# Loading K of the first octet as two half-row transfers instead of one

## The chip, the cores and the metric

The kernel runs on one core of one Trainium2 chip. A core has a matrix engine (TensorE, PE in the profile), two engines for elementwise work (VectorE, DVE; ScalarE, ACT), a general engine (GpSimd, POOL), a synchronisation engine (SyncE, SP) and 16 DMA engines that move data between HBM and the on-chip SBUF. SP and POOL issue transfers; the DMA engines carry them out. The metric is the device time of one execution in microseconds (us), as the median of several runs.

## What is computed

Q, K and V have the shape 8 x 12 x 512 x 64 in float32: 96 heads of 512 rows of 64 numbers. Each head is a linear attention with ReLU features:

```python
Q_feat = np.maximum(0, Q)
K_feat = np.maximum(0, K)
KV = np.einsum('bhkd,bhkv->bhdv', K_feat, V)
K_sum = np.sum(K_feat, axis=2)
numerator = np.einsum('bhqd,bhdv->bhqv', Q_feat, KV)
denominator = np.einsum('bhqd,bhd->bhq', Q_feat, K_sum)
return (numerator / (denominator[:, :, :, None] + 1e-10)).astype(np.float32)
```

Each of Q, K, V and the output is 12.58 MB, so 37.75 MB are read and 12.58 MB written.

## The kernel before

**Tiles.** The 96 heads are cut into 12 octets of 8 heads (`NO = 12`). One octet of one tensor is 1 MB in float32 and is laid on 128 partitions, each of which gets one contiguous run of 32 rows (`RQ = 32`) of 64 numbers, which is 8 KB; a partition so holds rows of one head only, and a head covers 16 partitions.

**Loads.** The K and V of the first octet are loaded by SP as float32, into the tiles `k_first` and `v_first` (lines 105 to 109). They live in two buffers of the output pool (tag `o_sb`, 7 buffers), which is still empty then. Everything else is loaded by POOL, which converts to bfloat16 on the way: first Q of octet 0 (`load_q(0)`, line 110), then for each octet K, V and Q in this order (lines 113 to 127). Octets 1 to 8 (`N8 = 9`) are loaded in whole octets of 8 KB rows; K and V of the last three in halves of 4 KB rows (lines 125 and 126). All of POOL's loads are written at the start of its program; at most about eight of them are under way at once, since each one waits for an older one to land before it is issued.

**Work per octet.** `prep8_k` (line 155) takes the ReLU of one half of K on DVE and multiplies it by a mask, into two masked copies `kf`. `prep8_v` (line 161) writes masked copies of V to `vo_all`, partly on DVE (line 167) and partly on ACT (line 165). `mm_kv8` (line 169) multiplies the two on PE and accumulates over the 32 rows in PSUM; `evac_kv8` (line 179) copies the result to `kvd` on ACT. `qt` transposes Q on PE (line 224) and takes its ReLU on ACT (line 232). `denom` (line 271) makes the reciprocal of the denominators, `out_t` (line 246) the numerators, `back` (line 289) transposes them back, and `norm` (line 296) scales them on DVE into an `o_sb` tile that SP stores.

**Order.** The schedule is written by hand (`tc.manual_schedule()`): each engine runs its instructions in the order in which the code emits them, and the framework adds only the waits. On DVE the start is: the constant parts of `vo_all` (`zero8`, lines 145 and 147), the masks made from the identity matrix (lines 332 to 337), zeroing `kvd` (line 150), `zero_masks` (lines 132 to 135), and then, for both halves i of the first octet (lines 341 to 344):

```python
for i in range(2):
    prep8_k(0, i)
    prep8_v(0, i, 0, nc.vector)
    prep8_v(0, i, 1, nc.scalar)
```

`prep8_k(0, 0)` reads rows 0 to 15 of `k_first` on every partition, `prep8_k(0, 1)` rows 16 to 31; between the two stands `prep8_v(0, 0, 0)`, which reads `v_first`.

**Stores.** `store` (line 304) holds each store back: SP first issues a tiny transfer (a "probe", line 307) that reads from the K tile of the octet five further on (`DELAY = 5`), so it can only go out when that tile has landed, and then the store itself (line 315). The last octet's output goes out in two halves (line 313). The probes begin with the landing of octet 5, and so for the first third of the time the DMA engines only load.

Of the kernel before, what the change touches and what calls it, by code (L numbers as in the profile page):

```python
# [10 lines left out]
def kernel(  # L11
# [7 lines left out]
    nc = tc.nc  # L19
    B, H, S, D = Q.shape  # L20
# [6 lines left out]
    R = S * 4 // P  # L27
# [30 lines left out]
    def view(X, f):  # L58
        return X.rearrange("b h s d -> (b h s d)").rearrange("(n p f) -> n p f", p=P, f=f)
# [45 lines left out]
    K8, V8 = view(K, RQ * D), view(V, RQ * D)  # L105
    k8 = outp.tile([P, RQ, D], fp32, name="k_first", tag="o_sb")
    v8 = outp.tile([P, RQ, D], fp32, name="v_first", tag="o_sb")
    nc.sync.dma_start(out=k8.rearrange("p r d -> p (r d)"), in_=K8[0])
    nc.sync.dma_start(out=v8.rearrange("p r d -> p (r d)"), in_=V8[0])
    load_q(0)  # L110
    make_identity(nc, ident)
# [331 lines left out]
```

## Time and profile before

| what | value |
|---|---|
| three runs, median (lowest to highest) | 127.08 us (126.86 to 127.38) |
| the profiled execution, its own time | 127.24 us |
| its span, first to last instruction | 125.5 us |
| mean granted TensorE clock | 0.94 |
| busy: PE, DVE, ACT, POOL | 85.0, 82.0, 83.6, 23.5 us |
| DMA time on POOL's queue, as a share of 16 engines' span | 72.1% |
| DMA time on SP's queue, same measure | 28.8% |
| HBM traffic | 37.75 MB read, 12.58 MB written |
| issue to landing, median: V of the first octet | 9.4 us |
| issue to landing, median: Q, and whole K octets on POOL | 20.3 and 21.3 us |

The profiled execution took 127.24 us, of which 125.5 us lie between its first and last instruction; the 1.74 us around it are launch and end. Times inside the profile are counted from the span's start. A "window" row of the trace gives, for one stretch of time, the busy time of each engine with the number of its instructions, the granted PE clock, the mean busy share of the 16 DMA engines (which overlaps of consecutive packets carry a little above 1), and the rate in GB/s. That rate counts the bytes written at the destination: a POOL load reads 2 bytes of float32 for each byte of bfloat16 that it writes, so 213 GB/s there are 426 GB/s read. A timeline row gives start, duration, engine, line, operation, tiles and shape, and in square brackets how long the engine sat idle before it and what ended that.

### The profile page before, as it was taken

How to read it: one execution, taken by the hardware profiler on the slowest of the kernel's cores; microseconds unless marked ns; L12 is line 12 of the kernel's file. 1: busy time of each engine (PE TensorE's matmuls, PEld its weight loads, DVE VectorE, ACT ScalarE, POOL GpSimd, SP SyncE). 2: the span in 40 equal slices, each digit the busy share in tenths (PEclk: the TensorE clock that was granted, in tenths of full speed). 3: DMA queues.
4: the chain of work that ended last, by engine and by line, in shares of the span. 5: the costliest groups of instructions: out<-in, count | busy, mean ns of one | idle time of the engine just before them, and what ended most of it. 6: DMA issues, size and time to landing. Idle time of an engine off the chain costs nothing.

```text
span 125.5 us, 3277 instructions
## 1 busy us (share of the span) xinstructions
PE 85.0 (68%) x1363; PEld 76.0 (61%) x1363; DVE 82.0 (65%) x187; ACT 83.6 (67%) x146; POOL 23.5 (19%) x46
## 2 busy tenths in 40 slices
PE   0005829987879878798784995694497499597800
PEld 0005828966759667696672893593494498496700
DVE  2826519399594995949769337957909806988630
ACT  0006998899797997989967846966659446646300
POOL 6901131112311131011121111133111000000000
PEclk9999995999999999999999589999999959999975
DMA  3999999999999999999999999999999999999991
GB/s 99 376 319 218 214 217 217 208 214 215 212 216 212 214 217 235 316 222 253 323 230 239 320 242 227 356 210 249 338 212 232 334 233 219 359 411 428 431 384 63
DMA packets 8047, 32.72 MB, mean 261 GB/s; under 512 B 992, under 2 KB 992, under 8 KB 6368
## 3 DMA queue, kind: packets, MB, share of 16 engines
q0 software_dynamic: 5760, 17.83, 72.1%
q1 hardware_dynamic: 2272, 14.69, 28.8%
q8 instruction: 10, 0.16, 0.5%
q14 instruction: 5, 0.04, 0.1%
HBM read 37.75 MB, written 12.58 MB: 401 GB/s over the span
## 4 chain that ended last, share of the span: by engine, by line
DVE 31%; PE 28%; DMA 27%; issue 4%; ACT 4%; DVEq 1%; SPq 0%; ACTq 0%
DMA v_oct<-in_V_dram 19%; DVE o_sb L298 15%; PE ps_kv L173 9%; PE ps_bk L292 8%; DMA v_first<-in_V_dram 7%; PE ps_kv L203 4%; PE ps_qt L224 3%; DVE kf L189 2%; DVE own L277 2%; DVE den L282 2%; DVE kf L158 2%; DVE rec L286 2%; ACT kvd L183 2%; DVE vo_all L191 2%; PE ps_ot L254 1%
## 5 line engine op out<-in xcount | busy, mean ns | idle before, releaser
L298 DVE TENSOR_TENSOR o_sb<-ps_bk,rec 128x1024 f32<-128x1024 f32 x24 | 28.3, 1219 | 17.1 <-PE ps_bk L292 17.1
L224 PE MATMUL ps_qt<-ident,q_sb 128*128 128x128 bf16 x192 | 15.6, 247 | 12.3 <-DMA q_sb<-in_Q_dram 12.3
L173 PE MATMUL ps_kv<-vo_all,kf 64*128 64x132 bf16 x288 | 20.2, 229 | 5.2 <-DVE vo_all L167 4.8
L256 ACT COPY ot_sb<-ps_ot 128x1024 f32<-128x1024 f32 x22 | 21.5, 1015 | 3.3 <-PE ps_ot L254 3.0
L292 PE MATMUL ps_bk<-ident,ot_sb 128*128 128x128 f32 x192 | 23.4, 275 | 0.0
L173 PEld LDWEIGHTS <-kf 64*128 64x128 bf16 x576 | 18.7, 100 | 6.7 <-DVE vo_all L167 5.8
L232 ACT ACTIVATE qt<-ps_qt 128x1024 bf16<-128x1024 bf16 x23 | 22.4, 1031 | 0.5 <-PE ps_qt L224 0.4
L224 PEld LDWEIGHTS <-q_sb 128*128 128x128 bf16 x192 | 14.2, 113 | 12.9 <-DMA q_sb<-in_Q_dram 12.5
L292 PEld LDWEIGHTS ps_bk<-ident,ot_sb 128*128 128x128 f32 x192 | 20.9, 141 | 0.9
L173 PE MATMUL ps_den<-vo_all,kf 64*128 64x132 bf16 x288 | 20.2, 229 | 0.0
L158 DVE TENSOR_SCALAR kf<-k_oct,mask8k 128x1024 bf16<-128x1024 bf16 x32 | 13.4, 459 | 5.8 <-DMA k_oct<-in_K_dram 5.8
L254 PE MATMUL ps_ot<-qt,kvd 128*128 128x256 bf16 x88 | 13.6, 284 | 4.1 <-DVE o_sb L298 3.9
L183 ACT CAST kvd<-ps_kv 64x130 bf16<-64x130 f32 x36 | 9.5, 265 | 6.8 <-PE ps_den L173 6.1
L274 PEld LDWEIGHTS <-qt 128*128 128x128 bf16 x192 | 6.8, 97 | 9.2 <-issue 7.9
L254 PEld LDWEIGHTS <-kvd 128*128 128x128 bf16 x88 | 8.2, 101 | 6.8 <-issue 5.8
L274 PE MATMUL ps_den<-kvd,qt 128*128 128x16 bf16 x192 | 7.3, 179 | 7.2 <-ACT kvd L183 6.5
L213 ACT CAST kvd<-ps_kv 64x260 bf16<-64x260 f32 (+1 forms) x14 | 4.6, 328 | 9.0 <-PE ps_kv L203 8.4
L102 POOL DMA_DIRECT2D q_sb<-in_Q_dram x12 | 7.0, 584 | 18.5 <-DMA k_oct<-in_K_dram 12.6
L165 ACT ACTIVATE vo_all<-v_oct,mask 128x1024 bf16<-128x1024 bf16 x8 | 9.2, 1154 | 1.8 <-DMA v_oct<-in_V_dram 1.6
L203 PE MATMUL ps_kv<-vo_all,kf 128*128 128x132 bf16 x96 | 7.5, 237 | 4.1 <-DVE vo_all L198 3.6
L167 DVE TENSOR_SCALAR vo_all<-v_oct,mask 128x1024 bf16<-128x1024 bf16 x24 | 10.2, 481 | 0.0
L183 ACT CAST kvd<-ps_den 64x130 bf16<-64x130 f32 x36 | 9.5, 265 | 0.8
(40 smaller groups left out, 70.7 us busy)
## 6 DMA issues: line engine op xcount, KB each, us to landing
out_dram<-o_sb SPq DMA_DIRECT2D x11, 1024.0 KB, 9.0
q_sb<-in_Q_dram POOLq DMA_DIRECT2D x12, 512.0 KB, 20.3
k_oct<-in_K_dram POOLq DMA_DIRECT2D x8, 512.0 KB, 21.3
v_oct<-in_V_dram POOLq DMA_DIRECT2D x8, 512.0 KB, 20.3
k_oct<-in_K_dram POOLq DMA_DIRECT2D x6, 256.0 KB, 17.9
v_oct<-in_V_dram POOLq DMA_DIRECT2D x6, 256.0 KB, 16.9
k_first<-in_K_dram SPq DMA_DIRECT2D x1, 1024.0 KB
v_first<-in_V_dram SPq DMA_DIRECT2D x1, 1024.0 KB, 9.4
```

The lines of the kernel that those rows point to most:

```text
L158: nc.vector.tensor_scalar(kf[2 * o + i][:, :, s, :], kb[o][:, R * i:R * i + R], scalar1=0.0, scalar2=mask8k[:, s:s + 1], op0=Alu.max, op1= ...
L167: nc.vector.tensor_scalar(to, vb[o][:, rows], scalar1=mask[:, 0, t:t + 1], scalar2=None, op0=Alu.mult)
L173: nc.tensor.matmul(ps_row[i], kf[2 * o + r // R][ps, r % R, :, :].rearrange("p s d -> p (s d)"), vo8[o % 2][ps, r, :, 1:D4 - 1], start=(r ...
L183: nc.scalar.copy(kvd[o % NK][64 * c:64 * c + 64, 4 * i + s:4 * i + 4:2, c * D1:c * D1 + D1], ps_row[i][64 * s:64 * s + 64, :, c:c + D1])
L203: nc.tensor.matmul(ps_kv[:, g % 2, 0:2 * (D + 2)].rearrange("p (t d) -> p t d", t=2), kf[g][:, r, :, :].rearrange("p s d -> p (s d)"), vo[ ...
L224: nc.tensor.transpose(ps[:, u, :], q_sb[o][:, i * (U // 2) + u, :], ident)
L232: nc.scalar.activation(to, ps, Act.Relu)
L254: nc.tensor.matmul(ps[:, i], kvd[o % NK][:, h, 1:2 * D + 1], q[:, :, h, :], start=True, stop=True, skip_group_check=True)
L256: nc.scalar.copy(ot[o][:, :, 4 * j:4 * j + 4], ps.rearrange("p h u c -> p u h c"))
L274: nc.tensor.matmul(ps[:, u], qt_sb[o % NZ][:, u, :], kvd[o % NK][:, :, 0:2 * D1:2 * D1 - 1], start=True, stop=True, skip_group_check=True)
L292: nc.tensor.transpose(ps[:, 2 * v:2 * v + 2].rearrange("p c d -> p (c d)"), ot[o][:, 8 * j + v].rearrange("p h c -> p (h c)"), ident32)
L298: nc.vector.tensor_tensor(o_sb[:, rs], ps, rec[o][:, rs].unsqueeze(2).to_broadcast([P, 16, D]), op=Alu.mult)
```

## The change

K of the first octet is loaded by two transfers on SP. The first brings the first 4 KB of every partition's 8 KB (rows 0 to 15), the second the last 4 KB (rows 16 to 31). V follows as a third transfer on the same queue, in whole 8 KB rows as before. The tile, its place and all other instructions stay as they are.

```diff
-    nc.sync.dma_start(out=k8.rearrange("p r d -> p (r d)"), in_=K8[0])
+    for i in range(2):
+        rs = slice(R * D * i, R * D * i + R * D)
+        nc.sync.dma_start(out=k8.rearrange("p r d -> p (r d)")[:, rs], in_=K8[0][:, rs])
     nc.sync.dma_start(out=v8.rearrange("p r d -> p (r d)"), in_=V8[0])
     load_q(0)
```

`R * D` is 16 x 64 = 1024 numbers, or 4 KB.

## The prediction

> **What bounds the kernel now.** I read the 40 slices first. Each digit is the busy share of the 16 DMA engines in tenths; the numbers under it are GB/s at the destination.
>
> ```profile
> DMA  3999999999999999999999999999999999999991
> GB/s 99 376 319 218 214 217 217 208 214 215 212 216 212 214 217 235 316 222 253 323 230 239 320 242 227 356 210 249 338 212 232 334 233 219 359 411 428 431 384 63
> HBM read 37.75 MB, written 12.58 MB: 401 GB/s over the span
> ```
>
> The DMA engines are full from the second slice to the last but one, while no compute engine is busy for more than 68% of the span. The windows give the full rate (GB/s is the last column, DMA share the one before):
>
> ```profile
> 4.00:4.90 0.90, 0.00 (x0) 0.00 (x0) 0.83 (x4) 0.00 (x0) 0.90 (x3) 1.00 1.06 437
> 16.00:40.00 24.00, 18.96 (x347) 16.80 (x347) 16.50 (x35) 21.29 (x40) 5.37 (x10) 0.93 1.06 213
> 82.00:83.90 1.90, 1.90 (x46) 1.79 (x41) 0.97 (x3) 0.91 (x4) 0.74 (x1) 1.00 1.13 211
> 108.00:118.00 10.00, 8.66 (x119) 8.23 (x119) 8.10 (x18) 5.35 (x10) 0.00 (x0) 1.00 1.02 422
> 121.00:122.00 1.00, 0.00 (x0) 0.00 (x0) 0.00 (x0) 0.00 (x0) 0.00 (x0) 0.50 1.05 426
> ```
>
> Row 1 is SP's float32 load alone (437), row 2 POOL's loads of 8 KB rows (213 written, so 426 read), row 3 POOL's loads of 4 KB half rows (211, so 422 read), row 4 stores in 8 KB rows (422), row 5 the last store, in 4 KB rows (426). So all forms run at about 425 GB/s. The 37.75 + 12.58 = 50.33 MB need 118.1 us at 426 GB/s; the traffic lies between about 1.8 and 124.1 us, 122.3 us. The sum of DMA work is the bound, and its first and last 2 us are the only places where it is thin.
>
> The chain of waits says something else, and I don't follow it: it has "DMA v_oct" for 24.27 us from 59.51 on, and DVE and PE around it. Those 24 us are a queue of some eight transfers of about 2.5 us, so throughput again, and DVE's own rows show that compute caught up with the loads well before the end:
>
> ```profile
> 63.98 0.89 DVE L158 TENSOR_SCALAR kf<-k_oct,mask8k 128x1024 bf16<-128x1024 bf16 x2 [2.13 <-DMA k_oct<-in_K_dram]
> 73.86 0.88 DVE L158 TENSOR_SCALAR kf<-k_oct,mask8k 128x1024 bf16<-128x1024 bf16 x2 [3.67 <-DMA k_oct<-in_K_dram]
> 82.60 0.88 DVE L189 TENSOR_SCALAR kf<-k_oct,mask 128x1024 bf16<-128x1024 bf16 x2 [0.85 <-DMA k_oct<-in_K_dram]
> 83.81 0.49 DVE L191 TENSOR_SCALAR vo_all<-v_oct,mask 128x1024 bf16<-128x1024 bf16 x1 [0.33 <-DMA v_oct<-in_V_dram]
> ```
>
> DVE waits here for K of octets 7, 8 and 9 to land. A compute chain that starts up to 2.13 us later reaches 63.98 at the same time, and up to 2.13 + 3.67 = 5.80 us later it is level again at 73.86. The stores up to there hang on the probes, thus on landings, too.
>
> Now the start, where the change is:
>
> ```profile
> 0.74 0.39 SPq L108 DMA_DIRECT2D k_first<-in_K_dram  x1
> 1.19 0.42 SPq L109 DMA_DIRECT2D v_first<-in_V_dram  x1
> 1.24 0.66 POOL L102 DMA_DIRECT2D q_sb<-in_Q_dram  x1 [0.79 <-POOLq L427]
> 5.53 0.06 DVE L135 MEMSET mask<- 64x1 f32 x1
> 5.64 1.42 DVE L158 TENSOR_SCALAR kf<-k_first,mask8k 128x1024 bf16<-128x1024 f32 x2
> 10.60 0.75 DVE L167 TENSOR_SCALAR vo_all<-v_first,mask 128x1024 bf16<-128x1024 f32 x1 [3.54 <-DMA v_first<-in_V_dram]
> ```
>
> The first reader of K (L158 at 5.64) starts 0.05 us behind the last mask MEMSET (5.53 + 0.06 = 5.59) and shows no wait. By the trace's records of single DMA packets, which no view lists, K's packets run from 1.76 to 5.27 us, V's from 4.93 to 10.27, and Q's first one starts at 5.34. DVE then waits 3.54 us for V.
>
> **The change part by part.**
>
> *K's first half lands earlier: worth nothing.* Half of K would land near 4 us instead of 5.3. DVE has MEMSETs until 5.59, so at most 5.64 - 5.59 = 0.05 us could go, and then DVE would wait for V 0.05 us longer. The second half is first read by `prep8_k(0, 1)`, which stands behind the V work of 10.60 on DVE. Its new wait is met some 5 us earlier; behind it are queued the second V copy on DVE and, through `kf`, the second half of PE's products. I set it at 0, at most 0.05 us, covered by the 2.13 us at 63.98.
>
> *One more issue on SP.* It costs 0.39 us of SP's time, and V's issue moves from 1.19 to about 1.63. Nothing else stands on SP until the probe at 43.57, and POOL's queue is its own. V's issue would end near 2.05. K's first packets came 0.6 to 1.5 us behind the end of K's issue (1.13, to 1.76 and, on the last engine, 2.65), so V's would be ready between 2.7 and 3.6; K holds the engines until about 5. That is a cover of 1.4 us. The second K half is ready between 2.2 and 3.1; the first one holds the engines until about 3.7 (data flow from about 2.5, then 0.5 MB at 437 GB/s is 1.2 us). Cover: 0.6 us. So 0, with each us of a hole costing one us, since the DMA work is the bound.
>
> *128 rows become 256.* Each engine handles 16 pieces of 4 KB instead of 8 of 8 KB. The trace has no such load; the bounds come from its neighbours. Stores: 426 in 4 KB rows against 422, so nothing or a gain of 1%. POOL's loads: 211 against 213, so a loss of 1%. One MB at 426 GB/s is 2.46 us, so that is -0.02 to +0.02 us. By the packets' own records the loss is larger: 173 ns for a half row against 324 ns for a whole one is 22 ns for every extra piece, times 8 is 0.18 us; but these records overlap, and the window rate does not bear them out. Gains at the bottom end: a shorter first piece could bring the first data half a packet (309 ns / 2) earlier, -0.15. I take +0.03 (the loss of the nearest load, 0.02, and the 16 extra completion writes, one of 9 ns per engine); ends -0.15 and +0.18.
>
> *V beside Q.* From 5.34 on V and Q take turns, one packet each, so a K that ends 0.03 later puts V's end 0.03 to 0.06 later, and if V loses one turn on one engine, a Q packet of 0.32. DVE and PE then start up to 0.4 us later. That is under the 2.13 us of cover at 63.98: nothing. Without that cover it would be up to 0.4 us.
>
> A rule of the Trainium skill speaks against the change: "DMA: Bandwidth & Descriptors", section "Rules for kernel authors", advises at least 1 MiB in a DMA, and the section "Anatomy of one DMA" there gives a fixed cost of about 2.0 us for each. Were that paid in the queue, the sum would be about 2 us more. The trace speaks against paying it: V's first packets run at 4.93 us while K's last are still under way. "Perfetto Trace Analysis", section "DMA Optimizations", says for splitting that it may help if the DMA engines are generally idle; here they are not.
>
> *Sum.* +0.03 on the profiled execution's 127.24 gives 127.27. That execution lies 0.16 above the median of the three runs, 127.08; on the median I forecast 127.1.
>
> **The rivals.**
>
> *Slower: a hole in the DMA work at the start.* If the second half's pieces, or V's, come to the engines only when the transfer ahead is done, the engines stand idle between. Place: 3.7 us, and again at 5. Price: one us for each us, and the lag from issue to packets, 0.6 to 1.5 us, is the measure: 127.7 to 128.6. It decides when the lag of the second transfer exceeds its cover by over 0.6 us, that is beyond 1.2 us on all engines. For it: only four engines had packets at 1.76, the rest between 2.28 and 2.65, so the descriptor delivery is not instant. Against it: V followed K without a gap.
>
> *Faster: the engines end more evenly.* At the end the DMA engines aren't done together:
>
> ```profile
> 122.00:123.00 1.00, 0.00 (x0) 0.00 (x0) 0.00 (x0) 0.00 (x0) 0.00 (x0) 0.50 0.66 266
> 123.00:124.10 1.10, 0.00 (x0) 0.00 (x0) 0.00 (x0) 0.00 (x0) 0.00 (x0) 0.50 0.14 56
> ```
>
> By the packet records eight of them finish at 122.5 us, the last at 124.07, 1.2 us behind the mean. If smaller pieces at the start shift the turns so that the last engine has less to catch up, up to 1.2 us go: 125.9 to 126.5. Against it: every engine gets the same 8 rows of each transfer before and after, and nothing at 5 us reaches that imbalance by a mechanism I can name.
>
> *The split does nothing at all* (the first reader waits for neither half anyway): 127.1, the forecast's own number; it can't be told from it by time.
>
> **How the numbers follow.** Forecast, including the split that does nothing: 0.70, with its own range from 127.08 - 0.15 - 0.22 = 126.7 to 127.08 + 0.18 + 0.30 = 127.6 (the bounds, and the spread of the three runs). Hole: 0.17. Even end: 0.13. 0.5% is 0.64 us, about what a measurement of this kernel can tell from no change; below 126.45 is faster, above 127.72 slower. The two rivals lie beyond these marks, the forecast within. To hold 8 in 10, the range must reach a little into both rivals: 126.5 to 127.9.
>
> **What would show it.** In the changed profile SP should have three issues near 0.74, 1.19 and 1.64; L158 should still start at 5.6 with no wait; L167 should wait for V until 10.6 to 11.0; the windows from 3 to 5 us should be at 410 to 440 GB/s without a dip at 3.7 (a dip is the hole); the wait at 63.98 should shrink by what V lost, and the landing at 83.8 should stay within 0.2 us. I am wrong if DVE's wait for octet 7 is gone, if GB/s between 2.5 and 5 falls, or if the last packets end over 0.6 us from 124.07.

## The result, and the profile after

The changed kernel takes 127.68 us (median of 7 runs, 127.52 to 128.01), the kernel before 127.09 us in the same comparison (7 runs, 126.86 to 127.38). The ratio is 1.0048, with a 95% interval of [1.0035, 1.006]: 0.6 us slower, at the edge of the 0.5% that the prediction took for the limit of what can be told, and inside its range of 126.5 to 127.9. The forecast was 127.1. The profiled execution of the changed kernel took 127.68 us, with a span of 125.9; that of the kernel before took 127.24, so the two traces are 0.44 us apart. Ratios leave out executions more than 1.5% above the fastest of their kernel; only e9_quarters_block below has any, two of six.

The DMA engines' slices of the page after:

```profile
DMA  3999999999999999999999999999999999999981
GB/s 109 312 318 255 211 213 217 215 208 213 217 213 211 215 216 235 318 224 257 320 228 246 316 237 228 354 212 244 336 215 226 343 230 213 374 415 422 416 363 79
HBM read 37.75 MB, written 12.58 MB: 400 GB/s over the span
```

They are as full as before. The one number that changes much at the start is the second slice (3.1 to 6.3 us), 312 GB/s where the kernel before has 376. The windows cut this finer; first before, then after (the last two columns are DMA share and GB/s):

```profile
1.70:2.50 0.80, 0.00 (x0) 0.00 (x0) 0.22 (x2) 0.00 (x0) 0.72 (x4) 1.00 0.67 123
2.50:3.00 0.50, 0.00 (x0) 0.00 (x0) 0.26 (x2) 0.00 (x0) 0.50 (x2) 1.00 0.71 295
3.00:4.00 1.00, 0.00 (x0) 0.00 (x0) 0.91 (x5) 0.00 (x0) 1.00 (x2) 1.00 0.97 410
4.00:5.00 1.00, 0.00 (x0) 0.00 (x0) 0.90 (x6) 0.00 (x0) 1.00 (x3) 1.00 1.08 442
```

```profile
1.70:2.50 0.80, 0.00 (x0) 0.00 (x0) 0.22 (x2) 0.00 (x0) 0.72 (x4) 1.00 0.64 220
2.50:3.00 0.50, 0.00 (x0) 0.00 (x0) 0.26 (x2) 0.00 (x0) 0.50 (x2) 1.00 0.96 254
3.00:4.00 1.00, 0.00 (x0) 0.00 (x0) 0.91 (x5) 0.00 (x0) 1.00 (x2) 1.00 0.95 246
4.00:5.00 1.00, 0.00 (x0) 0.00 (x0) 0.90 (x6) 0.00 (x0) 1.00 (x3) 1.00 1.03 410
```

After the change the data begin to flow sooner (220 against 123), but from 2.5 to 4 us they come at 254 and 246 instead of 295 and 410, and the shares of 0.96 and 0.95 say that the engines are busy all the while: the pieces take longer. In the trace's records of single packets (which no view lists) 34 of 75 pieces take 250 to 500 ns there; before 2.4 us most take 160 to 200 ns, after 3.7 us 159. So the slow stretch ends with the first half of K: 128 pieces have started by 3.93 us, and the second half, at the same pitch of 8 KB, runs at full speed (410 from 4 to 5 us).

The start of the changed kernel in the timeline:

```profile
0.74 0.86 SPq L110 DMA_DIRECT2D k_first<-in_K_dram  x2
1.64 0.43 SPq L111 DMA_DIRECT2D v_first<-in_V_dram  x1
5.60 1.42 DVE L160 TENSOR_SCALAR kf<-k_first,mask8k 128x1024 bf16<-128x1024 f32 x2
11.69 0.75 DVE L169 TENSOR_SCALAR vo_all<-v_first,mask 128x1024 bf16<-128x1024 f32 x1 [4.67 <-DMA v_first<-in_V_dram]
```

K's first reader starts at 5.60, 0.04 us sooner, and the V work at 11.69, which is 1.09 us later. DVE's later waits for transfers:

```profile
74.18 0.88 DVE L160 TENSOR_SCALAR kf<-k_oct,mask8k 128x1024 bf16<-128x1024 bf16 x2 [1.48 <-DMA k_oct<-in_K_dram]
82.87 0.88 DVE L191 TENSOR_SCALAR kf<-k_oct,mask 128x1024 bf16<-128x1024 bf16 x2 [0.79 <-DMA k_oct<-in_K_dram]
84.10 0.49 DVE L193 TENSOR_SCALAR vo_all<-v_oct,mask 128x1024 bf16<-128x1024 bf16 x1 [0.35 <-DMA v_oct<-in_V_dram]
```

The wait at 63.98 is gone. The three landings that DVE still waits for come 0.32, 0.27 and 0.29 us later than before. At the end:

```profile
122.00:123.00 1.00, 0.00 (x0) 0.00 (x0) 0.00 (x0) 0.00 (x0) 0.00 (x0) 0.50 0.98 401
123.00:124.10 1.10, 0.00 (x0) 0.00 (x0) 0.00 (x0) 0.00 (x0) 0.00 (x0) 0.50 0.35 138
124.10:125.50 1.40, 0.00 (x0) 0.00 (x0) 0.00 (x0) 0.00 (x0) 0.00 (x0) 0.50 0.02 9
```

The last packet ends at 124.57 instead of 124.07 us. So a lag of 0.3 us that arises before 7 us is carried through the whole kernel, and some 0.2 us come on top at the end.

### The profile page after: what moved, and what is told of

Same layout as the page of the kernel before. It is cut to its first block, busy times and chain, and to the rows that moved or that the text cites. A ratio compares the mean times of both kernels' runs of the same rounds, so it can differ in the third digit from the quotient of the medians.

```text
span 125.9 us, 3279 instructions
## 1 busy us (share of the span) xinstructions
PE 87.0 (69%) x1363; PEld 77.5 (62%) x1363; DVE 82.0 (65%) x187; ACT 83.3 (66%) x146; POOL 23.1 (18%) x46
## 4 chain that ended last, share of the span: by engine, by line
DMA 57%; PE 19%; DVE 12%; ACT 4%; issue 2%; DVEq 1%; SPq 1%; ACTq 0%
DMA k_oct<-in_K_dram 35%; DMA q_sb<-in_Q_dram 14%; DMA v_first<-in_V_dram 8%; DVE o_sb L300 7%; PE ps_kv L175 6%; PE ps_bk L294 5%; PE ps_qt L226 2%; PE ps_kv L205 2%; ACT kvd L185 2%; PE ps_ot L256 1%; ACT L167 1%; PE ps_den L175 1%; ACT vo_all L167 1%; DVEq L440 1%; DVE den L284 1%
## 5 line engine op out<-in xcount | busy, mean ns | idle before, releaser
L175 PE MATMUL ps_kv<-vo_all,kf 64*128 64x132 bf16 x288 | 21.0, 234 | 6.9 <-DVE vo_all L169 5.6
L175 PEld LDWEIGHTS <-kf 64*128 64x128 bf16 x576 | 19.5, 102 | 8.4 <-DVE vo_all L169 7.0
L294 PE MATMUL ps_bk<-ident,ot_sb 128*128 128x128 f32 x192 | 24.4, 282 | 0.0
L294 PEld LDWEIGHTS ps_bk<-ident,ot_sb 128*128 128x128 f32 x192 | 21.8, 146 | 0.9
L226 PE MATMUL ps_qt<-ident,q_sb 128*128 128x128 bf16 x192 | 14.4, 235 | 11.3 <-DMA q_sb<-in_Q_dram 11.3
L175 PE MATMUL ps_den<-vo_all,kf 64*128 64x132 bf16 x288 | 21.0, 234 | 0.0
L226 PEld LDWEIGHTS <-q_sb 128*128 128x128 bf16 x192 | 13.0, 106 | 11.8 <-DMA q_sb<-in_Q_dram 11.5
L256 PE MATMUL ps_ot<-qt,kvd 128*128 128x256 bf16 x88 | 14.5, 296 | 3.0 <-DVE o_sb L300 2.6
L205 PE MATMUL ps_kv<-vo_all,kf 128*128 128x132 bf16 x96 | 8.0, 248 | 3.1 <-DVE vo_all L200 2.5
L205 PEld LDWEIGHTS <-kf 128*128 128x128 bf16 x96 | 7.4, 111 | 3.9 <-issue 1.6
```

The source lines that it names most:

```text
L175: nc.tensor.matmul(ps_row[i], kf[2 * o + r // R][ps, r % R, :, :].rearrange("p s d -> p (s d)"), vo8[o % 2][ps, r, :, 1:D4 - 1], start=(r ...
L205: nc.tensor.matmul(ps_kv[:, g % 2, 0:2 * (D + 2)].rearrange("p (t d) -> p t d", t=2), kf[g][:, r, :, :].rearrange("p s d -> p (s d)"), vo[ ...
L226: nc.tensor.transpose(ps[:, u, :], q_sb[o][:, i * (U // 2) + u, :], ident)
L256: nc.tensor.matmul(ps[:, i], kvd[o % NK][:, h, 1:2 * D + 1], q[:, :, h, :], start=True, stop=True, skip_group_check=True)
L294: nc.tensor.transpose(ps[:, 2 * v:2 * v + 2].rearrange("p c d -> p (c d)"), ot[o][:, 8 * j + v].rearrange("p h c -> p (h c)"), ident32)
```

## The experiments

All ran beside the kernel before on the same chip; times are medians, ratios are to that kernel. The columns between are read from one profiled execution each. "Lag" is worked out from the packet records: how many microseconds later than in the kernel before a given amount of data has been moved (POOL's loads counted at 2 bytes read for each byte written). "Last Q" is the landing of the last load of all, Q of octet 11: its issue on POOL plus the time to landing that the DMA view gives, as in these lines of the kernel before (the issue in its timeline, the landing in its DMA view) and then the changed one:

```profile
94.31 0.53 POOL L102 DMA_DIRECT2D q_sb<-in_Q_dram  x1 [0.96 <-PE ps_bk L292]
q_sb<-in_Q_dram POOLq DMA_DIRECT2D x1, 512.0 KB, 16.7
```

```profile
94.77 0.53 POOL L102 DMA_DIRECT2D q_sb<-in_Q_dram  x1 [1.02 <-DMA v_oct<-in_V_dram]
q_sb<-in_Q_dram POOLq DMA_DIRECT2D x1, 512.0 KB, 16.6
```

That is 111.0 before and 111.4 after.

| kernel | lag at 0.25 MB | at 2 MB | at 10 MB | V work on DVE | last Q | time | ratio [95%] |
|---|---|---|---|---|---|---|---|
| before | | | | 10.60 | 111.0 | 127.1 | |
| changed | -0.28 | 0.34 | 0.27 | 11.69 | 111.4 | 127.68 | 1.0048 [1.0035, 1.006] |
| e1_pitch | -0.55 | -0.35 | -0.37 | 11.53 | 111.0 | 127.49 | 1.0023 [1.0009, 1.0037] |
| e2_rows | 0.15 | 1.48 | 1.53 | 14.81 | 112.6 | 128.41 | 1.0105 [1.0085, 1.0124] |
| e3_one | 0.42 | 0.59 | 0.48 | 11.27 | 111.4 | 127.56 | 1.0034 [1.0022, 1.0047] |
| e6_dve_held | -0.07 | -0.04 | -0.12 | 12.81 | 111.0 | 127.09 | 1.0003 [0.9993, 1.0013] |
| before_short | 0.03 | -0.02 | -0.03 | | 111.0 | 127.10 | 0.9994 [0.9983, 1.0006] |
| after_short | -0.10 | 0.38 | 0.34 | | 111.4 | 127.76 | 1.0048 [1.003, 1.0066] |
| pitch_short | -0.42 | -0.31 | -0.28 | | 111.0 | 127.20 | 1.0011 [0.9997, 1.0025] |
| e10_tiny | 0.07 | 0.46 | 0.41 | 11.42 | 111.4 | 127.35 | 1.0013 [0.9999, 1.0027] |
| e8_quarters | -0.21 | 1.22 | 1.24 | 18.20 | 112.8 | 129.25 | 1.0164 [1.0151, 1.0178] |
| e9_quarters_block | -0.39 | 0.97 | 0.99 | 19.07 | | 127.72 to 128.60 (four runs) | 1.009 [1.0065, 1.0115] |
| e7_v_split | 0.04 | 0.57 | 0.89 | 10.07, 13.81 | 111.9 | 127.95 | 1.0064 [1.0051, 1.0076] |
| e11_extra | 0.00 | | | 10.65 | 112.2 | 128.29 | 1.0089 [1.0076, 1.0101] |

My theory at first was that reading half of every row, at a pitch of 8 KB, slows K ("pitch"). Its rivals: the pieces of 4 KB themselves ("pieces"), the third transfer on SP's queue ("transfers"), and V's lateness.

**e1_pitch.** Only the source of the two halves changes.

```diff
-        nc.sync.dma_start(out=k8.rearrange("p r d -> p (r d)")[:, rs], in_=K8[0][:, rs])
+        nc.sync.dma_start(out=k8.rearrange("p r d -> p (r d)")[:, rs], in_=Kr[i])
```

> The changed kernel with its two K transfers, but each reads one contiguous block of 512 KB from HBM (the first 4 heads, then the last 4) instead of 4 KB out of every 8 KB. Same bytes, same pieces of 4 KB, same three transfers; the tile then holds other rows of K per partition than the masks assume, so the first octet's numbers are not the reference's. In the changed kernel the DMA work lags by about 0.3 us from 7 us on (K of octet 8 lands at 74.18 against 73.86). Theory pitch (the 8 KB pitch in HBM slows the first half): no lag, V for DVE at 10.6, time 127.1. Theory pieces (256 pieces of 4 KB cost it) and theory transfers (a third transfer on SP's queue costs it): lag stays, V at 11.7, time 127.7.

```profile
1.70:2.50 0.80, 0.00 (x0) 0.00 (x0) 0.22 (x2) 0.00 (x0) 0.72 (x4) 1.00 0.89 251
2.50:3.00 0.50, 0.00 (x0) 0.00 (x0) 0.26 (x2) 0.00 (x0) 0.50 (x2) 1.00 0.98 377
3.00:4.00 1.00, 0.00 (x0) 0.00 (x0) 0.91 (x5) 0.00 (x0) 1.00 (x2) 1.00 1.03 401
```

The slow stretch is gone: 377 and 401 GB/s against 254 and 246. With the same pieces and the same three transfers, reading two solid blocks makes the DMA work lead by 0.35 us. So the slow reads come from reading 4 KB out of every 8 KB. Why only the first half suffers, though the second has the same pitch, isn't shown. V is as late as ever, so that has another cause:

```profile
11.53 0.75 DVE L169 TENSOR_SCALAR vo_all<-v_first,mask 128x1024 bf16<-128x1024 f32 x1 [4.51 <-DMA v_first<-in_V_dram]
```

The median is 127.49, not 127.1 or less. The twelve runs fall into two groups, five from 126.97 to 127.16 and seven from 127.45 to 127.67. The profiled one, 127.16, is of the lower group: its time is that of the kernel before, its lead doesn't reach the end, and its last Q lands at 111.0 as before. No trace shows an execution of the upper group. So it isn't shown that the slow reads are the whole cost of the change: without them most runs are still 0.4 us longer.

**e2_rows.** Two transfers of whole rows.

```diff
-        rs = slice(R * D * i, R * D * i + R * D)
-        nc.sync.dma_start(out=k8.rearrange("p r d -> p (r d)")[:, rs], in_=K8[0][:, rs])
+        ps = slice(64 * i, 64 * i + 64)
+        nc.sync.dma_start(out=k8.rearrange("p r d -> p (r d)")[ps], in_=K8[0][ps])
```

> K in two transfers of 64 partitions each, in whole 8 KB rows: 128 pieces of 8 KB as before, three transfers as in the changed kernel. Theory transfers: V's pieces still come to the engines late, Q goes first, V for DVE at about 11.7, time 127.7. Theories pieces and pitch: like the kernel before, V at 10.6, time 127.1.

V came at 14.81 and the time was 128.41, worse than any theory said. The window from 3 to 4 us shows 221 GB/s at a DMA share of 1.01, with K almost alone (two pieces of Q): a transfer onto 64 partitions ran at about half the rate of one onto 128. This run has a cost of its own and decides nothing about the third transfer.

**e3_one.** One transfer, 256 pieces.

```diff
-    nc.sync.dma_start(out=k8.rearrange("p r d -> p (r d)"), in_=K8[0])
+    nc.sync.dma_start(out=k8p[:, :, 0:R], in_=K8[0].rearrange("p (i r d) -> p i r d", i=2, d=D))
```

(`k8p` is a tile of [P, 2, R + 1, D] that `prep8_k` reads for octet 0.)

> K in one transfer whose destination has a gap after each 4 KB, so that it is cut into 256 pieces of 4 KB; two transfers in all, as before. Theory pieces: V late (11.7) and time 127.7, as in the changed kernel. Theory transfers: V at 10.6 and 127.1. Theory pitch: the pieces are read in pairs that are neighbours in HBM, so 127.1.

```profile
2.50:3.00 0.50, 0.00 (x0) 0.00 (x0) 0.26 (x2) 0.00 (x0) 0.50 (x2) 1.00 0.18 33
3.00:4.00 1.00, 0.00 (x0) 0.00 (x0) 0.91 (x5) 0.00 (x0) 1.00 (x2) 1.00 0.91 360
4.00:5.00 1.00, 0.00 (x0) 0.00 (x0) 0.90 (x6) 0.00 (x0) 1.00 (x3) 1.00 1.07 442
```

The pieces run at full rate once they run (442), so 4 KB pieces as such are not slow. This transfer starts late instead (33 GB/s at a share of 0.18), its issue taking 0.68 us of SP instead of 0.39. The lag of 0.42 at 0.25 MB is there from the first data on, and the time is 0.45 us longer: the first clean case of a loss at the start that comes back whole at the end. No theory had foreseen this start; "pieces" had the sign of the time and of V's lateness, for another reason.

**e6_dve_held.** No transfer changes; DVE is kept busy.

```diff
         prep8_k(0, i)
+        if i == 0:
+            for _ in range(9):
+                nc.vector.memset(hold, 0.0)
         prep8_v(0, i, 0, nc.vector)
```

> The kernel before, with nine MEMSETs of 520 numbers on DVE (about 4.7 us) behind the first ReLU of K, so that the V work on DVE starts at about 11.7 instead of 10.6, as it does in the changed kernel, while no transfer changes. Theory: the compute start is free (DVE waits 2.1 + 3.7 us for K of octets 7 and 8): 127.1, K of octet 8 at 73.9. Rival: V's lateness itself is what costs, through PE's later start: 127.4 to 127.7.

```profile
12.81 0.63 DVE L168 TENSOR_SCALAR vo_all<-v_first,mask 128x1024 bf16<-128x1024 f32 x1
73.80 0.88 DVE L159 TENSOR_SCALAR kf<-k_oct,mask8k 128x1024 bf16<-128x1024 bf16 x2 [2.90 <-DMA k_oct<-in_K_dram]
```

127.09 against 127.11, ratio 1.0003 [0.9993, 1.0013], and K of octet 8 at 73.80. The MEMSETs held DVE longer than meant: its V work starts at 12.81, 2.2 us late, and the first scaling of an output at 26.42 against 25.12. DVE's wait at 63.98 shrinks to 0.65 and the next one to 2.90, and the time stays. A late compute start of this size costs nothing. In the changed kernel the first scaling is 3.0 us late (28.16), more than here; how 1.09 us at V become 3.0 there wasn't followed. But DVE still has 1.48 us to wait for K of octet 8, so its cover isn't used up either.

**before_short, after_short, pitch_short.** The changed kernel's profile had a stretch of half clock from 108 to 111 us, and its last store went out 0.76 us later than before (119.81 against 119.05). To see whether the last octet's compute adds to the time, a piece of it is left out in three kernels.

```diff
-    mm_kv(g + 1)
-    evac_kv(o + 1, slice(1, 2), share=True)
```

> The kernel before without the last half octet's K-V product and its evacuation (mm_kv(g + 1) and evac_kv of slice 1 to 2), so that heads 4 to 7 of the last octet are made from older values; every transfer stays. This takes some 2 us out of the last octet's compute. Theory: before ends on its DMA work alone, so 126.9 to 127.1, at most 0.2 faster. Rival (its last stores wait for compute): 126.0 or less.

> The changed kernel with the same piece of the last octet left out. Theory (two parts): the DMA work is 0.3 us late from 7 us on, and the other 0.3 us of the 0.6 us come from the last octet's compute, hit by a stretch of half clock at 108 to 111 us, so that the last store is issued at 119.8 instead of 119.0; with the compute shortened 0.3 us remain: 127.2 to 127.4, K of octet 8 still at 74.2. Rival (all 0.6 us is DMA work): 127.6.

> The kernel with the two contiguous K blocks (first octet's rows mixed up) and the same piece of the last octet left out. Its DMA work was 0.3 us ahead of the kernel before until 119 us, and its time yet 0.4 longer. Theory: the loss is the last octet's compute; without it the lead shows, 126.6 to 126.9. Rival: the lead is lost elsewhere, 127.1 to 127.5.

before_short: 127.10, no difference. after_short: 127.76, and its profile has the last store at 117.91, almost 2 us sooner than the changed kernel's, with the last packet at 124.53 against 124.57. So my theory of two parts falls: the last octet's compute is no part of the changed kernel's 0.6 us. pitch_short: 127.20 (e1_pitch 127.49), but not because each run got shorter: nine of twelve lie between 127.07 and 127.28 and three between 127.49 and 127.70, so the two groups of e1_pitch are still there, with more runs in the lower one. Whether the shorter compute moved them isn't shown. The lead of 0.3 us doesn't show in either.

**e10_tiny.** A third transfer that moves almost nothing.

```diff
+    nc.sync.dma_start(out=tiny, in_=K8[0][:, 0:16])
     nc.sync.dma_start(out=v8.rearrange("p r d -> p (r d)"), in_=V8[0])
```

> The kernel before with a small third transfer on SP between K and V: 64 bytes on each of 128 partitions into a tile that nobody reads. Theory transfers (a third transfer ahead makes V's pieces late at the engines, so that Q goes first): V for DVE at 11 or later. Theory pieces (only K's own pieces matter): V at 10.6. For the time both say 127.1 to 127.2, since a late V is free; 127.5 and more would say that a third transfer costs by itself.

```profile
4.00:5.00 1.00, 0.00 (x0) 0.00 (x0) 0.90 (x6) 0.00 (x0) 1.00 (x3) 1.00 1.02 415
5.00:6.00 1.00, 0.00 (x0) 0.00 (x0) 0.66 (x9) 0.00 (x0) 1.00 (x3) 1.00 0.83 207
```

V is at 11.42, with K untouched: a third transfer on SP is enough to make it late, and here the engines stand idle for a moment (share 0.83 from 5 to 6 us). By the packet records K's last piece ends at 5.28 us, and the first sixteen pieces of V (one for each engine) start from 5.43 to 6.13; in e1_pitch K ends at 4.94 and they start from 5.25 to 6.10. In the kernel before they follow K at once, from 4.93 to 5.24. So the third transfer isn't ready when K is done, and Q's pieces go first. V's issue ends near 2.08, 3.2 to 3.4 us ahead of its first piece; that isn't the transfer's own lag, since V queues behind K (in the kernel before it is 3.3 us too, from 1.61 to 4.93). The time is 0.2 us longer, with an interval that just takes in no change.

**e8_quarters and e9_quarters_block.** K in four transfers of 2 KB rows, at the pitch and as blocks.

```diff
-    for i in range(2):
-        rs = slice(R * D * i, R * D * i + R * D)
+    for i in range(4):
+        rs = slice(R * D // 2 * i, R * D // 2 * (i + 1))
```

(e9 has `in_=Kq[i]` beside this, with `Kq = view(K, RQ * D // 4)`.)

> K in four transfers of 2 KB quarter rows, each piece 8 KB from the next in HBM: twice the pieces and twice the number of passes over the same 1 MB, compared with the changed kernel. Theory pitch (reading part of every row, at a pitch of 8 KB, is what slows K): the windows from 2.5 to 5 us fall further than in the changed kernel (254 and 246 GB/s at 2.5 to 4), the DMA work lags by 0.5 us or more, 127.8 to 128.4. Theory startup (only the first transfer's first pieces suffer, whatever their number): 127.6 to 127.7 as in the changed kernel.

> K in four transfers of 2 KB rows too, but each reads one contiguous block of 256 KB (the tile then holds other rows of K per partition than the masks assume, so the first octet's numbers are not the reference's). Theory pitch: K runs at 380 GB/s or more from 2.5 us on, and K of octet 8 lands at 73.9 or earlier; time 127.0 to 127.6. Theory pieces (the number of pieces or of transfers ahead of V costs): as slow as the quarter rows at a pitch.

The quarter rows at the pitch, and then the blocks:

```profile
3.00:4.00 1.00, 0.00 (x0) 0.00 (x0) 0.91 (x5) 0.00 (x0) 1.00 (x2) 1.00 1.04 188
4.00:5.00 1.00, 0.00 (x0) 0.00 (x0) 0.90 (x6) 0.00 (x0) 1.00 (x3) 1.00 0.98 180
```

```profile
3.00:4.00 1.00, 0.00 (x0) 0.00 (x0) 0.91 (x5) 0.00 (x0) 1.00 (x2) 1.00 1.28 291
4.00:5.00 1.00, 0.00 (x0) 0.00 (x0) 0.90 (x6) 0.00 (x0) 1.00 (x3) 1.00 0.73 135
```

Both windows hold pieces of Q, which count half at the destination, and a window counts a piece whole where it starts. In bytes read, by the packet records, it is 209 and 258 GB/s at the pitch and 356 and 254 with the blocks. From 3 to 4 us a 2 KB piece of K takes 157 ns on average at the pitch and 96 with the blocks: the reads at the pitch are slow here too, which fits "pitch", while part of the loss is idle time (cut at the window's edges, the engines are 0.79 busy from 3 to 3.5 us). Over all its pieces the second quarter is the slow one, 170 ns a piece against 94 with the blocks; the first takes 97. The time of e8, 129.25, is above the 128.4 that this theory allowed. e9 went against what "pitch" alone said (380 and more) and shows the second cause, the transfers: K's second quarter ends at 3.85 us and the third quarter's first piece starts at 4.65, 2.6 us behind the end of its issue (2.07) with nothing of its queue ahead of it; until then only Q's pieces run. The profiled execution of e9 took 130.81 us, so only its start is used. In both, the third and fourth quarter take 3.7 to 4.7 us each by the packet records, since they share the engines with Q piece by piece: a 2 KB piece of K waits for a whole 8 KB row of Q. V then comes 7.6 us late in e8 (18.20), more than the 5.80 us of cover; no wait of DVE for a transfer is left from there to 85 us, and the time rises by 2.1 us, more than the lag of 1.24 and the 1.8 us by which the last Q is late.

**e7_v_split.** K whole, V in two half rows.

```diff
-    nc.sync.dma_start(out=v8.rearrange("p r d -> p (r d)"), in_=V8[0])
+    for i in range(2):
+        rs = slice(R * D * i, R * D * i + R * D)
+        nc.sync.dma_start(out=v8.rearrange("p r d -> p (r d)")[:, rs], in_=V8[0][:, rs])
```

> K whole as in the kernel before, V in two transfers of 4 KB half rows at a pitch of 8 KB. Theory pitch: the slow reads come back in V's part, 5 to 10 us, and the DMA work lags by 0.2 to 0.4 us: 127.3 to 127.7. Theory startup (only transfers right at the start suffer): no lag, 127.1 to 127.2.

The lag is 0.04 until V's part and grows to 0.89 within it; the time is 127.95. By the packet records the engines read 360 GB/s from 6 to 10 us, against 422 in the kernel before, and 412 against 430 from 10 to 12 us, when the second half of V runs. So the slow reads are not a matter of the kernel's start, and again they lie in the first half. V's last piece begins at 13.0 us instead of 9.6, for the reason seen in e8: 4 KB of V now wait for 8 KB of Q. The engines are not all full either, by the packet records down to 0.92 in the half microsecond from 7.5. The theory had the sign and half of the size.

**e11_extra.** A price for added work: half a MB more behind V.

```diff
     nc.sync.dma_start(out=v8.rearrange("p r d -> p (r d)"), in_=V8[0])
+    nc.sync.dma_start(out=extra, in_=Kr[0])
```

> The kernel before with an additional SP load of 512 KB behind V, one contiguous block into a tile that nobody reads. It is a price for DMA work added at the start: at 425 GB/s it takes 1.23 us of all engines. Theory (the sum of DMA work is the bound, 1 to 1): 128.3, K of octet 8 at 75.1. Rival (the start has slack, the end is set by compute or by something that does not move): 127.1 to 127.6.

```profile
75.03 0.88 DVE L160 TENSOR_SCALAR kf<-k_oct,mask8k 128x1024 bf16<-128x1024 bf16 x2 [3.68 <-DMA k_oct<-in_K_dram]
```

128.29, which is 1.16 us more for 1.23 us of work; K of octet 8 lands 1.17 us later. Here one us of the DMA engines at the start costs one us at the end.

## Why the prediction was right or wrong

The number lies in the stated range only because the range was stretched into the rivals: the forecast's own range ended at 127.6, and 127.68 is nearly the lower end of the hole, 127.7. Two terms of the sum were wrong.

**What bounds the kernel: right.** The DMA work sets the time, one to one (e11_extra, e3_one), and compute has cover (e6_dve_held, before_short). One refinement: it is not the mean over the 16 engines. Compared execution by execution, the time goes with the landing of the last Q, that is with the slowest engine, within 0.2 us in the twelve other kernels of the table, e9_quarters_block left out: in the profiled executions 0.4 us later give 0.44 in the changed kernel, and 0.3, 0.8, 1.1, 1.6 and 1.8 us give 0.29, 0.85, 1.09, 1.50 and 1.96 in e3_one, e7_v_split, e11_extra, e2_rows and e8_quarters, while e1_pitch has 0.0 and -0.08. In e1_pitch and pitch_short 15 engines finish that load ahead of the kernel before (the second to last at 108.7 against 109.4 in e1_pitch) and the last one at 110.66 in both kernels, and the lead is lost.

**K's first half early: right.** It was worth 0.04 us at its reader; no gain from it shows at the end.

**256 pieces, the term that failed.** I put it at +0.03, with ends of -0.15 and +0.18, from rows of half-row transfers elsewhere in the trace. Those rows (211 against 213, 426 against 422) are of transfers whose half rows are neighbours in HBM; the changed load reads 4 KB out of every 8 KB, and no row of the trace had that. Measured: the first pieces come sooner, -0.28 at 0.25 MB, beyond my lower end; the slow stretch then takes 0.6 us back; 0.3 us remain at 2 MB, beyond the upper end. e1_pitch shows that it is this pattern of reading and e3_one that it is not the size of the pieces; that the second half at the same pitch runs at full rate says that the pitch alone does not explain it.

**One more issue on SP, wrong in its cover.** I had V's pieces ready between 2.7 and 3.6 us, from the lag of the first transfer. e9_quarters_block shows a third transfer whose first piece starts 2.6 us behind the end of its issue, not 0.6 to 1.5, and in e1_pitch and e10_tiny V isn't ready when K is done. The 1.4 us of cover was not there; V lost its turns to Q and came 1.09 us late, not up to 0.4. That a late V costs nothing by itself was right: e6_dve_held shows it for a first scaling that is 1.3 us late, and for the 3.0 us of the changed kernel the 1.48 us of waiting that are left say the same. Where the engines stand idle meanwhile, as in e10_tiny, it can cost. The fixed 2 us of the Trainium skill's "DMA: Bandwidth & Descriptors" ("Anatomy of one DMA", a fit for transfers that GpSimd issues, while these are SP's) were not paid on top: the whole change cost 0.6.

**The hole, the slower rival.** Its price, one us for each us, is the one that e11_extra shows. Its place was right in part: the dip is at 2.5 to 3.7 us, and the one that it had at 5 us is not there. The mechanism was not: the engines are busy and the reads long. It came to 0.3 us of work and 0.6 us of time, the low end of the 0.6 to 1.5 I gave it. "The engines end more evenly" did not happen.

**The signs to look for.** Two of the three that I named against myself came true: GB/s between 2.5 and 5 fell, and DVE's wait for octet 7 is gone. The third did not, but only just: the last packet is 0.5 us later, with a limit of 0.6. Of the signs for the forecast, V's start (11.69 against 10.6 to 11.0) and the landing at 83.8 (0.29 us later against 0.2) failed.

**What stays open.** The changed kernel's lag is 0.3 us on the mean engine and 0.4 at the last Q. Its time is 0.44 us longer between the two traces and 0.6 between the medians, since the profiled execution of the kernel before lies 0.15 above its median; where the other executions lose or gain this, no trace tells. after_short excludes the last octet's compute. Why the reads at the pitch are slow in a part of a load alone (the first half here, the second quarter in e8_quarters), and what sets the upper group of e1_pitch, is open. Nor is it shown why the slowest engine of e1_pitch does not keep its lead. The packet records hold ten instruction fetches of 16 KB, each about 0.9 us long, and a landing's last engine falls 1 us behind the others near such a fetch (22.20 to 22.57 for fifteen engines and 23.56 for the last, with a fetch at 21.8, in the kernel before); that these choose the engine that ends last is a guess that wasn't tried.

## What to carry to other kernels

Where the DMA engines are full from start to end, look at GB/s in windows of a microsecond, not at who waits: DMA work lost at the start, where nobody waits for it, came back at the end about one to one. If a load must be split, let each transfer read a solid block of HBM over all 128 partitions: cutting rows into columns cost read rate here, and each smaller piece still gave up its turn to a whole piece of the other queue. Even the solid blocks gained nothing here. Compare a trace with the time of its own execution, not with the median. A cost taken from a row of the trace holds only for the same access pattern, not just for the same size.

## What the runs showed of the hardware

- Parts of rows at a pitch of 8 KB were read slowly for a stretch: from 3 to 4 us 246 GB/s in 4 KB pieces and 209 in 2 KB pieces (Q's reads counted in full), against 410 for whole rows and 401 for 4 KB rows of a solid block. From 4 to 5 us, with the second half at the same pitch, the changed kernel was back at 410.
- A third transfer on SP's queue is ready late. In e9_quarters_block its first piece starts 2.6 us behind the end of its issue and 0.8 us behind the last piece ahead of it; the first transfer's starts 0.6 us behind its issue. V as the third starts 0.2 to 0.3 us and more behind K's last piece, whether the second moves 512 KB (e1_pitch) or 8 KB (e10_tiny); as the second it follows at once.
- SP's and POOL's queues take turns by pieces, whatever their size: K's 2 KB pieces and Q's 8 KB rows alternate, and 256 KB of K take 3.7 to 4.7 us (e8_quarters, e9_quarters_block). The Trainium skill ("DMA: Bandwidth & Descriptors", section "Queues, rings and completion order") lets an engine drain a packet of some 9 to 17 descriptors before it switches; these runs show a switch after each row.
- A transfer onto 64 partitions ran at 221 GB/s where one onto 128 ran at 410. The same page's "Rules for kernel authors" advise against two transfers onto partition halves since they run one after the other; e2_rows agrees with the advice, and its loss of 1.5 us is more than one after the other would give, which at full rate is none.
- A transfer with a gap in its destination every 4 KB (e3_one) had its first 0.25 MB moved 0.42 us later than the whole one.
